# First MLP product as seven block products of block sums, in units of 256 features

## The chip, the cores and the metric

One core of a Trainium2 chip runs the whole program: TensorE (PE) multiplies, VectorE (DVE), ScalarE (ACT) and GpSimd (POOL) work beside it, SyncE (SP) issues the loads. The metric is the device time of one execution in microseconds (us); less is better.

## What is computed

One layer of a hybrid encoder on 512 tokens of 2048 features, in float32:

```python
hn = rms_norm(h, norm_mix_g)
u = hn @ w_pw1 + b_pw1                       # 2048 -> 4096
a, gate = split(u); u = a * sigmoid(gate)
u = depthwise_conv(u, w_dw, width 31) + b_dw
h = h + silu(layer_norm(u)) @ w_pw2 + b_pw2  # 2048 -> 2048
h = h + square(relu(rms_norm(h, norm_ffn_g) @ w_up)) @ w_down   # 2048 -> 8192 -> 2048
out = rms_norm(h, final_norm_g)
```

The change is in the product with `w_up`.

## The kernel before

Features lie on the 128 partitions and tokens along the free axis, so a product is made of matmuls with a 128 x 128 stationary block of weights and 512 moving tokens. For accuracy each float32 operand is split in two parts, `hi` (rounded) and `lo` (the rest), and each block product is three matmuls (`mm3`, L141 to L144): `wh*xh`, `wh*xl`, `wl*xh`. Each of the three has a weight load of its own.

Weights come as a stream of pieces of 512 KB (`pieces`), each 128 partitions x 1024 numbers. `fetch` issues the load of a piece on SP into a buffer `wr`; `split_hi` makes `wh` on ACT (L126), `split_lo` makes `wl` on DVE (L131). The pool has four buffers each of `wr`, `wh` and `wl`. `prep(upto)` does both for all pieces below `upto`.

Phase 1 (to about 390 us) is the first norm, the first pointwise product, the convolution and the LayerNorm. Phase 2 is the second pointwise product and the MLP. There the work is cut into calls of `group`: four output tiles of 128 features in four PSUM banks, over `nk` contraction tiles, two of them per piece, so a piece is 24 matmuls of 512 tokens. Groups use the two halves of the eight banks by turns. While piece p is multiplied, pieces up to p + 2 have been asked for.

After each of the four groups of the second pointwise product, per output tile k: DVE adds the residual (`h`, L781), ACT and DVE split `h` times the gain into `g{k}h` and `g{k}l` (L235, L236), ACT squares `h` (L791), and POOL adds the square to `Q2` (L795). From `Q2` come the token scales `r2` of the norm (`ffn_sum`, `ffn_scale`), which are applied to the product afterwards.

The MLP runs in eight chunks of 1024 hidden features. In each, two groups of 16 contraction tiles give 8 tiles of the hidden layer (relu times `r2` on DVE L818, square on ACT L822, `zh` on ACT L825, `zl` on DVE L826); then four groups of 8 contraction tiles go through `w_down`, and DVE adds each bank to `h` (L837). The last group of the last chunk goes over one half of the tokens and then over the other (`split`), in matmuls of 256 tokens, so that one half's final norm runs under the other's products.

The order on PE is written out by hand. The order on DVE, ACT, POOL and SP in phase 2 is left to a planner: it works with estimated durations, and of the instructions that are ready when an engine comes free it takes the one that is earliest in the program.

Of the kernel before, what the change touches and what calls it, by code (L numbers as in the profile page):

```python
# [24 lines left out]
# columns of the packed per-channel vectors  # L25
# [5 lines left out]
# order and shares of the work among the engines; depthwise taps by ScalarE and GpSimd, and by TensorE; VectorE takes the others  # L31
# [15 lines left out]
FF_CHUNK = 1024  # L47
# [4 lines left out]
def conformer_layer(ctx: ExitStack, tc: tile.TileContext, xT, vecs, wdw, w1, w2, wup, wdn, outT):  # L52
# [4 lines left out]
    wpool = ctx.enter_context(tc.tile_pool(name="wpool", bufs=4))  # L57
# [4 lines left out]
    vec = const.tile([P, 144], F32, name="vec")  # L62
    wd = const.tile([P, NK, CW], F32, name="wd")
# [13 lines left out]

    def col(base, k):
        return vec[:, base + k : base + k + 1]

# [14 lines left out]
    for c in range(DFF // FF_CHUNK):  # L95
        for g in range(FF_CHUNK // 512):
            for k in range(0, NK, 2):
                wide(wup, k * P, c * FF_CHUNK + g * 512)
        for g in range(4):
            for k in range(0, FF_CHUNK // P, 2):  # L100
                wide(wdn, c * FF_CHUNK + k * P, g * 512)

# [15 lines left out]

    def split_hi(i):
        shape = pieces[i][1]  # L120
        r = raws[i]
        pool, bufs = (ph1, 1) if i == n_p1 else (wpool, 4)
        hi = pool.tile(shape, F32R, tag="wh", name=f"wh{i}", bufs=bufs)
        lo = pool.tile(shape, F32R, tag="wl", name=f"wl{i}", bufs=bufs)
        prepped[i] = (hi, lo)
        nc.scalar.copy(out=hi, in_=r)  # L126
# [35 lines left out]
    def spread(dg, out, start=True):  # L162
        """[128 tokens, n] on partitions -> PSUM [128, n * 128], the same on every partition."""
# [20 lines left out]
    def rms_scale(b, name, pool, n=4):  # L184
        """1 / root mean square, tokens on partitions, from the mean squares in b"""
# [6 lines left out]
    # =================== phase 1: norm, pointwise, GLU, depthwise ===================  # L192
# [15 lines left out]
    # the first output pair's operands come, and are split, by contraction tile  # L208
    nc.scalar.dma_start(out=vec, in_=vecs)
    for i in range(4):  # L210
        raws[i] = wpool.tile(pieces[i][1], F32, tag="wr", name=f"wr{i}")
        prepped[i] = tuple(wpool.tile(pieces[i][1], F32R, tag=t, name=f"{t}{i}") for t in ("wh", "wl"))
    state["raw"] = state["prep"] = 4
    for k in range(NK):
# [26 lines left out]
    # The first PRE output pairs take x times the gain, and the norm's scale afterwards; the  # L241
    # others take the normalized x, which is ready by then.
# [3 lines left out]
    # squares of some tiles and their sum by GpSimd, of the others by ScalarE and VectorE  # L246
# [49 lines left out]
    def pw1(j, t0=0, n=T, more=False, hooks=None):  # L296
        pa, pg = bank("mm", f"pa{j}_{t0}")[:, 0:n], bank("mm", f"pg{j}_{t0}")[:, 0:n]
        for k in range(0, NK, 4):
# [3 lines left out]
            for kk in range(4):  # L302
# [3 lines left out]
                if j == 0:  # L306
                    # in the order in which the parts come
# [92 lines left out]
    def early(banks0, banks1):  # L400
        """the normalized x, with the first pairs' GLU and the first convolution between"""
# [33 lines left out]
    def conv_pe(acce, t0, n, i0, i1, npe):  # L435
        """taps i0.. of the npe last ones, of the last tile, on TensorE"""
# [518 lines left out]
```

## Time and profile before

| | |
|---|---|
| time, median of 3 runs | 1995.0 us (1994.71 to 1995.41) |
| span of the profiled execution | 1993.7 us |
| PE busy in the span | 1962.4 us, 98% |
| DVE, ACT, POOL busy | 968.8, 617.1, 387.9 us |
| weights and other data read | 193.27 MB, 99 GB/s with what is written |

The profiled execution has no time of its own beside its span; the median of the timed runs lies 1.3 us above that span. "Busy" counts the time in which an engine had an instruction in work. Matmuls are pipelined: the duration of one (0.39 us for 512 tokens) is longer than the distance from one start to the next, so the pace of PE is read from starts and counts.

### The profile page before, as it was taken

The page shows a single profiled execution, that of the slowest core. Times are in us where ns is not written, and L with a number is a line of the kernel's source. Part 1 is how long each engine was busy: PE and PEld are TensorE (multiplying, and loading weights), DVE is VectorE, ACT ScalarE, POOL GpSimd, SP SyncE. Part 2 cuts the span into 40 slices and gives each one's busy share as a digit, 9 for nine tenths or more (in the row PEclk, how much of TensorE's full clock was granted, in tenths as well). Part 3 has the DMA queues.
Part 4 walks back from the last instruction along what each step waited for, and adds up shares of the span by engine and source line. Part 5 has one row for each costly group of instructions (what it writes and reads, how often), then busy time and mean ns, then how long its engine had stood idle before and what let it go on. Part 6 is the DMA issues. An engine that isn't in the chain of part 4 may idle for free.

```text
span 1993.7 us, 21880 instructions
## 1 busy us (share of the span) xinstructions
PE 1962.4 (98%) x8888; PEld 1629.3 (82%) x8888; DVE 968.8 (49%) x1206; ACT 617.1 (31%) x799; POOL 387.9 (19%) x266
## 2 busy tenths in 40 slices
PE   8899999989999999999999999999999999999997
PEld 5788888978888888888888888888888888888887
DVE  7999999874443332333333233333323333332444
ACT  5533444553322212321221232122213212211332
POOL 6778899851210000000000000000000000000000
PEclk9999999999999999999999999999999999999998
DMA  7233333134233233223323322332332233233222
GB/s 218 76 102 97 92 98 96 54 110 154 96 98 92 99 100 98 95 95 96 98 101 97 95 95 96 97 102 97 96 96 95 96 99 101 95 96 95 96 95 85
DMA packets 155141, 198.88 MB, mean 100 GB/s; under 512 B 7328, under 2 KB 77216, under 8 KB 155040
## 3 DMA queue, kind: packets, MB, share of 16 engines
q1 hardware_dynamic: 154896, 197.42, 31.9%
q8 instruction: 69, 1.13, 0.2%
q14 instruction: 32, 0.26, 0.0%
q10 hardware_dynamic: 144, 0.07, 0.0%
HBM read 193.27 MB, written 4.19 MB: 99 GB/s over the span
## 4 chain that ended last, share of the span: by engine, by line
issue 70%; PE 24%; DVE 3%; DMA 1%; ACT 1%; SPq 0%; POOL 0%; POOLq 0%; DVEq 0%
PE g L143 3%; PE g L142 3%; PE g L144 3%; PE pa L144 2%; PE pa L143 2%; PE pg L144 2%; PE pg L143 2%; PE pg L142 2%; PE pa L142 2%; DMA wr<-w 1%; DVE sl L591 0%; DVE acc L373 0%; DVE wl L131 0%; DMA x<-xT 0%; PE acce L440 0%
## 5 line engine op out<-in xcount | busy, mean ns | idle before, releaser
L131 DVE TENSOR_TENSOR wl<-wr,wh 128x1024 fp32r<-128x1024 f32 x288 | 360.0, 1250 | 888.9 <-ACT wh L126 883.2
L126 ACT CAST wh<-wr 128x1024 fp32r<-128x1024 f32 x348 | 366.1, 1053 | 1175.9 <-PE g L143 1046.7
L142 PE MATMUL g<-zh,wh 128*128 128x512 f32 (+1 forms) x1056 | 404.3, 383 | 0.0
L143 PE MATMUL g<-zl,wh 128*128 128x512 f32 (+1 forms) x1056 | 404.0, 383 | 0.0
L144 PE MATMUL g<-zh,wl 128*128 128x512 f32 (+1 forms) x1056 | 404.0, 383 | 0.0
L189 POOL TENSOR_TENSOR rr_fin<-ms_fin,mhalf 128x2 f32<-128x2 f32 x2 | 1.4, 696 | 1374.2 <-DVE ms_fin L187 1374.2
L373 DVE SCALAR_TENSOR_TENSOR acc<-u,wd,acc 128x512 f32<-128x512 f32 (+1 forms) x362 | 237.4, 730 | 0.2
L142 PEld LDWEIGHTS g<-zh,wh 128*128 128x128 f32 x1056 | 198.4, 188 | 38.8
L143 PEld LDWEIGHTS g<-zl,wh 128*128 128x128 f32 x1056 | 198.4, 188 | 38.7
L144 PEld LDWEIGHTS g<-zh,wl 128*128 128x128 f32 x1056 | 198.4, 188 | 38.7
L131 POOL TENSOR_TENSOR wl<-wr,wh 128x1024 fp32r<-128x1024 f32 x60 | 145.9, 2431 | 40.1 <-ACT wh L126 40.0
L143 PE MATMUL g<-sl,wh 128*128 128x512 f32 (+1 forms) x288 | 107.1, 372 | 6.2 <-DVE sl L591 3.3
L142 PE MATMUL g<-sh,wh 128*128 128x512 f32 (+1 forms) x288 | 107.3, 373 | 0.0
L144 PE MATMUL g<-sh,wl 128*128 128x512 f32 (+1 forms) x288 | 106.3, 369 | 0.0
L837 DVE TENSOR_TENSOR h<-h,g 128x512 f32<-128x512 f32 x124 | 84.6, 687 | 40.8 <-PE g L144 40.8
L362 POOL TENSOR_TENSOR pc<-pc,pm 128x512 f32<-128x512 f32 (+1 forms) x65 | 79.7, 1227 | 3.6 <-ACT pm L360 1.2
L143 PEld LDWEIGHTS g<-sl,wh 128*128 128x128 f32 x288 | 55.2, 192 | 16.3 <-DVE sl L591 4.1
L142 PEld LDWEIGHTS g<-sh,wh 128*128 128x128 f32 x288 | 55.1, 191 | 9.2
L144 PEld LDWEIGHTS g<-sh,wl 128*128 128x128 f32 x288 | 55.3, 192 | 9.0
L360 ACT ACTIVATE pm<-u,wd 128x512 f32<-128x512 f32 (+1 forms) x82 | 53.1, 680 | 20.6 <-POOL pc L362 20.4
L822 ACT ACTIVATE z<-zt 128x512 f32<-128x512 f32 x64 | 40.3, 630 | 53.5 <-DVE zt L818 52.8
L818 DVE SCALAR_TENSOR_TENSOR zt<-g,r 128x512 f32<-128x512 f32 x64 | 43.9, 692 | 22.0 <-PE g L144 21.0
(907 smaller groups left out, 3383.5 us busy)
## 6 DMA issues: line engine op xcount, KB each, us to landing
wr<-wup SPq DMA_DIRECT2D x128, 512.0 KB, 3.8
wr<-wdn SPq DMA_DIRECT2D x128, 512.0 KB, 3.5
wr<-w SPq DMA_DIRECT2D x120, 256.0 KB, 3.3
wr<-w SPq DMA_DIRECT2D x32, 512.0 KB, 3.6
h<-xT SPq DMA_DIRECT2D x4, 1024.0 KB, 11.0
outT<-h SPq DMA_DIRECT2D x14, 256.0 KB, 2.8
x<-xT SPq DMA_DIRECT2D x6, 512.0 KB, 6.2
wr<-w SPq DMA_DIRECT2D x16, 128.0 KB, 5.4
```

Source lines behind the costliest of these rows:

```text
L126: nc.scalar.copy(out=hi, in_=r)
L131: eng.tensor_tensor(out=lo, in0=r, in1=hi.bitcast(F32), op=ALU.subtract)
L142: nc.tensor.matmul(out, lhsT=wh, rhs=xh, start=start, stop=False, **kw)
L143: nc.tensor.matmul(out, lhsT=wh, rhs=xl, start=False, stop=False, **kw)
L144: nc.tensor.matmul(out, lhsT=wl, rhs=xh, start=False, stop=stop, **kw)
L189: nc.gpsimd.tensor_tensor(out=r, in0=ms, in1=mhalf[:, 0:n], op=ALU.pow)
L360: nc.scalar.activation(out=pm, in_=u[:, c : c + n], func=AF.Copy, scale=wd[:, j, c : c + 1])
L362: nc.gpsimd.tensor_add(out=pn, in0=pc[-1], in1=pm)
L373: nc.vector.scalar_tensor_tensor(out=acc if c < end - 1 else vt, in0=u[:, c : c + n], scalar=wd[:, j, c : c + 1], in1=src, op0=ALU.mult, o ...
L818: nc.vector.scalar_tensor_tensor(out=t, in0=banks[m], scalar=0.0, in1=r2, op0=ALU.max, op1=ALU.mult)
L822: nc.scalar.activation(out=z, in_=t, func=AF.Square)
L837: nc.vector.tensor_add(out=h, in0=h, in1=banks[m])
```

## The change

The 2048 x 8192 weight of the first MLP product is worked on in 32 units of 256 hidden features. In each unit the output features, the contraction (pairs of contraction tiles) and the tokens are cut in halves, and the 2 x 2 x 2 block product is made of seven products of block sums and differences in place of eight. A unit has 8 pairs `kt` and for each 7 products, each three matmuls of 256 tokens.

- The sums of the activations are formed once, after the second pointwise product (`form`, `place`): for each of 8 pairs, four DVE operations of 256 columns, one ACT rounding and one DVE subtraction of 7 x 256 columns. They take the place of the split of each tile of `h`. The results for pairs 3 to 7 lie in the space of the second pointwise product's operands, so those for pairs 3 to 5 are written while group 3 runs, those for 6 and 7 behind it. The squares of `h` have one buffer, not two.
- The sums of the weights are formed for each piece (`split_blocks`): three DVE additions more, and the rounding and the subtraction are of 3 + 4 blocks, where they were of one piece. A piece takes two of the three buffers of `wh` and of `wl`; the pool has three buffers, not four (a fourth lives elsewhere in phase 1). The host hands the weights over in the order of the pieces.
- The outputs are put together from the seven products behind each unit (`up`): an ACT copy, four DVE operations that read PSUM, then relu and scale, square, split.
- A unit of the first product prepares one piece ahead (`prep(i0 + p + 2)`). Order: up 0, up 1, up 2, down (0, 1), up 3, up 4, down (2, 3), and so on to down (26, 27), up 29, 30, 31, down (28 to 31). `w_down` goes in 14 jobs of two units and one of four, so DVE adds the banks to `h` 15 times, where it was 8.

```diff
+WBUFS = 3
...
-    wpool = ctx.enter_context(tc.tile_pool(name="wpool", bufs=4))
+    wpool = ctx.enter_context(tc.tile_pool(name="wpool", bufs=WBUFS))
...
+    def split_blocks(i):
+        r = raws.pop(i)
+        s = wpool.tile(BLOCKS, F32, tag="ws", name=f"ws{i}", bufs=1)
+        hr, hs = (wpool.tile([P, 2, n, P], F32R, tag="wh", name=f"wh{i}_{n}", bufs=WBUFS) for n in (3, 4))
+        lr, ls = (wpool.tile([P, 2, n, P], F32R, tag="wl", name=f"wl{i}_{n}", bufs=WBUFS) for n in (3, 4))
+        prepped[i] = (hr, lr), (hs, ls)
+        nc.scalar.copy(out=hr, in_=r[:, :, 1:4])
+        nc.vector.tensor_tensor(
+            out=s[:, :, 0:2], in0=r[:, :, 1:3], in1=r[:, :, 0:1].to_broadcast([P, 2, 2, P]), op=ALU.add
+        )
+        nc.vector.tensor_add(out=s[:, :, 2], in0=s[:, :, 0], in1=r[:, :, 2])
+        nc.vector.tensor_add(out=s[:, :, 3], in0=s[:, :, 2], in1=r[:, :, 3])
+        nc.vector.tensor_tensor(out=lr, in0=r[:, :, 1:4], in1=hr.bitcast(F32), op=ALU.subtract)
+        nc.scalar.copy(out=hs, in_=s)
+        nc.vector.tensor_tensor(out=ls, in0=s, in1=hs.bitcast(F32), op=ALU.subtract)
...
+    OF_RAW = ((3, 3, 0), (6, 0, 0), (4, 1, 0))
+    OF_SUM = ((0, 3, 1), (2, 2, 1), (1, 1, 1), (5, 2, 0))
...
+    def form(kt, b):
+        t1, t2, t3, t4, b11, b12, b21, b22 = (b[:, i] for i in range(8))
+        nc.vector.tensor_sub(out=t3, in0=b12, in1=b22)
+        nc.vector.tensor_sub(out=t1, in0=b22, in1=b21)
+        nc.vector.scalar_tensor_tensor(out=t2, in0=t3, scalar=-1.0, in1=b21, op0=ALU.mult, op1=ALU.subtract)
+        nc.vector.tensor_add(out=t4, in0=t2, in1=b11)
+    def place(kt, b):
+        o = pair_operand(kt)
+        nc.scalar.copy(out=o[:, :, 0], in_=b[:, 0:7])
+        nc.vector.tensor_tensor(out=o[:, :, 1], in0=b[:, 0:7], in1=o[:, :, 0].bitcast(F32), op=ALU.subtract)
...
-                hi, lo = split_scaled(ph2, (f"b{2 * k}", f"b{2 * k + 1}"), f"g{k}", h, col(C_GFFN, k))
...
+            nc.scalar.activation(
+                out=blocks[:, at : at + 2].rearrange("p a b -> p (a b)"), in_=h, func=AF.Copy, scale=col(C_GFFN, k)
+            )
+            sq = ph2.tile([P, T], F32, tag="W", name=f"sqh{k}", bufs=1)
...
+        for p in range(4):
+            prep(i0 + p + 2)
+            for (wh, wl), of in zip(prepped.pop(i0 + p), (OF_RAW, OF_SUM)):
+                for kk in range(2):
+                    kt = 2 * p + kk
+                    for b, (x, q, half) in enumerate(of):
+                        out = banks[q][:, half * HT : half * HT + HT]
+                        xh, xl = T4_OF[kt][:, x, 0], T4_OF[kt][:, x, 1]
+                        first = kt == 0 and (of is OF_RAW or (q, half) == (2, 1))
+                        mm3(out, wh[:, kk, b], wl[:, kk, b], xh, xl, first, kt == 7, skip_group_check=True)
...
+        nc.scalar.copy(out=q1, in_=banks[0][:, 0:HT])
+        nc.vector.tensor_tensor(out=c[:, 2:6:2], in0=two(banks[1]), in1=bc(q1), op=ALU.add)
+        nc.vector.tensor_tensor(out=c[:, 3:6:2], in0=two(banks[2]), in1=bc(c[:, 4]), op=ALU.add)
+        nc.vector.tensor_tensor(out=c[:, 0:2], in0=two(banks[3]), in1=bc(c[:, 5]), op=ALU.subtract)
+        nc.vector.tensor_sub(out=c[:, 3], in0=c[:, 3], in1=banks[3][:, HT:T])
+        t = c[:, 0:4].rearrange("p (m a) t -> p m (a t)", m=2)
+        nc.vector.scalar_tensor_tensor(
+            out=t, in0=t, scalar=0.0, in1=r2[:, None, :].to_broadcast([P, 2, T]), op0=ALU.max, op1=ALU.mult
+        )
+        nc.scalar.activation(out=t, in_=t, func=AF.Square)
...
+        nc.scalar.copy(out=zh, in_=t)
+        nc.vector.tensor_sub(out=zl, in0=t, in1=zh.bitcast(F32))
```

## Rows read from the trace of the kernel before

**Rows 1.** Page, first part: busy us, share of the span, instructions.

```profile
PE 1962.4 (98%) x8888; PEld 1629.3 (82%) x8888; DVE 968.8 (49%) x1206; ACT 617.1 (31%) x799; POOL 387.9 (19%) x266
```

**Rows 2.** Stretches: length, busy us (count) by engine, PE clock, DMA share, GB/s.

```profile
610.00:1955.00 1345.00, 1345.00 (x5936) 1113.70 (x5935) 473.92 (x505) 338.78 (x392) 0.00 (x0) 1.00 0.31 96
1955.00:1984.00 29.00, 27.51 (x224) 27.03 (x222) 14.70 (x31) 12.11 (x26) 3.95 (x4) 0.99 0.22 73
```

**Rows 3.** Waits of PE, 440 to 1994 us, complete: total, times, longest.

```profile
PE sp_fin L164 <- DVE dg_fin L154: 1.5, 1, 1.5
```

**Rows 4.** Order of time on PE, 512 tokens: start, duration; first and last.

```profile
454.62 0.39 PE L143 MATMUL g<-sl,wh 128*128 128x512 f32 x1
...
499.04 0.39 PE L144 MATMUL g<-sh,wl 128*128 128x512 f32 x1
```

**Rows 5.** Order of time on PE, 256 tokens: two stretches, first and last of each.

```profile
411.13 0.28 PE L144 MATMUL g<-sh,wl 128*128 128x256 f32 x1
...
413.05 0.28 PE L142 MATMUL g<-sh,wh 128*128 128x256 f32 x1
...
1955.62 0.28 PE L142 MATMUL g<-zh,wh 128*128 128x256 f32 x1
...
1969.17 0.28 PE L144 MATMUL g<-zh,wl 128*128 128x256 f32 x1
```

**Rows 6.** Page, costliest groups, weight loads: busy us, mean ns, idle before.

```profile
L142 PEld LDWEIGHTS g<-zh,wh 128*128 128x128 f32 x1056 | 198.4, 188 | 38.8
```

**Rows 7.** Groups by line and shape on DVE, 800 to 1800 us.

```profile
L131 DVE TENSOR_TENSOR wl<-wr,wh 128x1024 fp32r<-128x1024 f32 x184 | 225.4, 1225 | 600.2 <-ACT wh L126 598.6
L837 DVE TENSOR_TENSOR h<-h,g 128x512 f32<-128x512 f32 x92 | 62.7, 687 | 30.2 <-PE g L144 30.2
L818 DVE SCALAR_TENSOR_TENSOR zt<-g,r 128x512 f32<-128x512 f32 x48 | 32.9, 692 | 16.5 <-PE g L144 15.8
L826 DVE TENSOR_TENSOR zl<-z,zh 128x512 fp32r<-128x512 f32 x48 | 31.9, 686 | 3.1 <-ACT zh L825 3.1
```

**Rows 8.** The same on ACT, 800 to 1800 us.

```profile
L126 ACT CAST wh<-wr 128x1024 fp32r<-128x1024 f32 x184 | 194.0, 1054 | 715.4 <-PE g L143 715.4
L822 ACT ACTIVATE z<-zt 128x512 f32<-128x512 f32 x48 | 30.2, 630 | 40.1 <-DVE zt L818 39.6
```

**Rows 9.** The same on DVE, whole span: a broadcast operand, and 256 columns.

```profile
L891 DVE TENSOR_TENSOR h<-h,sp_fin 128x512 f32<-128x512 f32 x12 | 7.3, 680 | 0.0
...
L858 DVE TENSOR_TENSOR Q<-Q,sqo 128x256 f32<-128x256 f32 x3 | 1.3, 419 | 0.0
```

**Rows 10.** The same on ACT, whole span: a copy of 256 columns from PSUM.

```profile
L550 ACT COPY mus<-acce 128x256 f32<-128x256 f32 x2 | 0.7, 372 | 5.4 <-PE acce L164 5.4
```

**Rows 11.** Order of time on DVE, behind the last group of the second pointwise product.

```profile
583.10 0.74 DVE L236 SCALAR_TENSOR_TENSOR g12l<-h,vec,g12h 128x512 fp32r<-128x512 f32 x1
...
584.42 1.12 DVE L236 SCALAR_TENSOR_TENSOR g13l<-h,vec,g13h 128x512 fp32r<-128x512 f32 x1
585.47 2.31 DVE L131 TENSOR_TENSOR wl<-wr,wh 128x1024 fp32r<-128x1024 f32 x1
587.70 1.78 DVE L236 SCALAR_TENSOR_TENSOR g14l<-h,vec,g14h 128x512 fp32r<-128x512 f32 x1
```

**Rows 12.** Order of time on POOL in the same stretch.

```profile
583.25 7.38 POOL L795 TENSOR_TENSOR Q<-Q,sqh 128x512 f32<-128x512 f32 x4 [36.13 <-ACT sqh L791]
```

**Rows 13.** Order of time on DVE, behind the first MLP group.

```profile
626.42 2.80 DVE L818 SCALAR_TENSOR_TENSOR zt<-g,r 128x512 f32<-128x512 f32 x4 [1.32 <-PE g L144]
629.14 0.68 DVE L826 TENSOR_TENSOR zl<-z,zh 128x512 fp32r<-128x512 f32 x1
629.95 1.23 DVE L131 TENSOR_TENSOR wl<-wr,wh 128x1024 fp32r<-128x1024 f32 x1
```

**Rows 14.** Waits in the queue of SP, whole span: total, times, longest.

```profile
SPq L115 <- DVE wl L131: 1442.5, 281, 35.9
```

**Rows 15.** Page, loads: count, KB each, median us from issue to landing.

```profile
wr<-wup SPq DMA_DIRECT2D x128, 512.0 KB, 3.8
```

More of the change, by code (lines that the diff above doesn't have):

```diff
@@ L76, in conformer_layer, with hl @@
     nc.vector.memset(mhalf, -0.5)
+    slots = [acts.tile([P, 7, T], F32R, name=f"slot{i}") for i in range(5)]
+    def hl(k):
+        return tuple(slots[n // 7][:, n % 7, :] for n in (2 * k, 2 * k + 1))
     def col(base, k):
@@ L94, in conformer_layer, with up_pieces, down_pieces @@
             wide(w2, k * P, g * 512)
[L95 to L98, printed above, removed]
-        for g in range(4):
-            for k in range(0, FF_CHUNK // P, 2):
-                wide(wdn, c * FF_CHUNK + k * P, g * 512)
+    BLOCKS = [P, 2, 4, P]
+    def up_pieces(u):
+        for p in range(4):
+            pieces.append((wupb[u, p], BLOCKS))
+    def down_pieces(units):
+        for g in range(4):
+            for u in units:
+                wide(wdn, u * UNIT, g * 512)
+    jobs = []
+    for u in range(N_UNITS):
+        jobs.append(("up", u))
+        if u % 2 == 0 and 2 <= u < N_UNITS - 2:
+            jobs.append(("down", (u - 2, u - 1)))
+    jobs.append(("down", tuple(range(N_UNITS - 4, N_UNITS))))
+    for kind, what in jobs:
+        (up_pieces if kind == "up" else down_pieces)(what)
     raws, prepped = {}, {}
@@ L210, in conformer_layer @@
     for i in range(4):
[L211 to L212 removed]
+        raws[i] = wtile(i, "wr", F32)
+        prepped[i] = wtile(i, "wh", F32R), wtile(i, "wl", F32R)
     state["raw"] = state["prep"] = 4
@@ L524, in conformer_layer @@
     mus = ph1.tile([P, T], F32, name="mus", bufs=1)
-    sh = [acts.tile([P, T], F32R, tag=f"a{2 * k}", name=f"sh{k}") for k in range(NK)]
-    sl = [acts.tile([P, T], F32R, tag=f"a{2 * k + 1}", name=f"sl{k}") for k in range(NK)]
+    sh, sl = zip(*(hl(k) for k in range(NK)))
     st = [{}, {}]
@@ L769, in conformer_layer @@
             hooks = dict(zip(LN_AT, (second_sums, second_mean, second_scale)))
+        if g == 3:
+            hooks = {(0, 2 + 2 * i, 0): (lambda kt: lambda: place(kt, blocks_of[kt]))(3 + i) for i in range(3)}
         banks = group(NK, sh, sl, hooks, split=4 if g == 0 else 0)
@@ L795, in conformer_layer @@
                 nc.gpsimd.tensor_add(out=Q2, in0=Q2, in1=sq)
+            if m % 2:
+                form(k // 2, blocks)
+                blocks_of[k // 2] = blocks
+                if k // 2 < 3 or g == 3:
+                    place(k // 2, blocks)
     r2 = const.tile([P, T], F32, name="r2")
@@ L836, in conformer_layer @@
+    Q3 = None
+    for kind, what in jobs[:-1]:
+        if kind == "up":
+            up(what)
+            continue
+        zh, zl = zip(*(t for u in what for t in z_of[u]))
+        for g in range(4):
+            banks = group(2 * len(what), zh, zl)
+            for m in range(4):
                 h = hT[g][:, m, :]
                 nc.vector.tensor_add(out=h, in0=h, in1=banks[m])
-                if end:
-                    sq = ph2.tile([P, T], F32, tag=f"b{k}", name=f"sqo{k}", bufs=1)
-                    nc.scalar.activation(out=sq, in_=h, func=AF.Square)
-                    nc.scalar.activation(out=h, in_=h, func=AF.Copy, scale=col(C_GFIN, k))
-                    if k == 0:
-                        nc.vector.tensor_copy(out=Q3, in_=sq)
-                    else:
-                        nc.vector.tensor_add(out=Q3, in0=Q3, in1=sq)
@@ L848, in conformer_layer, with sq_of @@
-    sqs = [ph2.tile([P, T], F32, tag=f"b{12 + m}", name=f"sqo{12 + m}", bufs=1) for m in range(4)]
+    last_units = jobs[-1][1]
+    zh, zl = zip(*(t for u in last_units for t in z_of[u]))
+    kc = len(zh)
+    Q3 = ph2.tile([P, T], F32, tag="Q2", name="Q3", bufs=1)
+    sqo = [ph2.tile([P, 7, T], F32, tag=f"T{i}", name=f"sqo{i}", bufs=1) for i in range(3)]
+    def sq_of(k):
+        return sqo[k // 7][:, k % 7, :]
+    for g in range(3):
+        banks = group(kc, zh, zl)
+        for m in range(4):
+            k = 4 * g + m
+            h = hT[g][:, m, :]
+            nc.vector.tensor_add(out=h, in0=h, in1=banks[m])
+            sq = sq_of(k)
+            nc.scalar.activation(out=sq, in_=h, func=AF.Square)
+            nc.scalar.activation(out=h, in_=h, func=AF.Copy, scale=col(C_GFIN, k))
+            if k == 0:
+                nc.vector.tensor_copy(out=Q3, in_=sq)
+            else:
+                nc.vector.tensor_add(out=Q3, in0=Q3, in1=sq)
@@ L850, in finish @@
+    sqs = [sq_of(12 + m) for m in range(4)]
     def finish(t0):
```

129 lines of the change are left out of this document (72 added, 57 removed).

## The prediction

> **What bounds the kernel now.** I read the page's first part, then stretches, then who waits. PE is busy for 98% of the span [rows 1], and in the MLP, from 610 to 1955 us, for all of it, at full clock; DVE works there 474 of 1345 us, ACT 339, POOL not at all, and the loads take 0.31 of the DMA engines [rows 2]. From 440 us to the end PE waited for another engine once, 1.5 us in the final norm [rows 3]. So the MLP lasts as long as its matmuls, and fewer of them shorten it as long as the others keep up. "Busy" hides the pace of one matmul. From starts: 44.42 us for 196 steps of 512 tokens, 0.2266 us each [rows 4], which the count of the long stretch repeats (1345 / 5936 = 0.2266) [rows 2]. In two stretches the kernel already runs matmuls of 256 tokens, each with its own weight load: 1.92 us for 16 steps, and 13.55 us for 113, 0.1199 us each [rows 5], while DVE and ACT are at work. Half of 0.2266 would be 0.1133: a half matmul costs 6.6 ns more than half.
>
> **The product.** Removed: 64 output tiles x 16 contraction tiles x 3 = 3072 matmuls, 3072 x 0.2266 = 696.1 us. Added: 32 units x 8 pairs x 7 products x 3 = 5376 of 256 tokens, 5376 x 0.1199 = 644.6 us. Gain 51.5 us, all on the path. Seven eighths would be 87; the price of the halves takes 36 of it. A unit lasts 168 x 0.1199 = 20.1 us, a piece 5.04 (18 matmuls with raw blocks 2.16, 24 with sums 2.88).
>
> A weight load is busy 188 ns by the page [rows 6], more than the step of 120 ns that I use; but each of those steps had one, so loads overlap [rows 5]. The Trainium skill, TensorE: Matmul & The Clock Gate, section Back-to-back issue gap, says that the spacing is set by load and matmul together, and gives 81 ns at 128 tokens and 131 at 512. By that a half matmul would cost (interpolated, an estimate) some three quarters of a whole one, and the product would take about 217 us more in place of 51 less. The trace does not agree: 0.1199 against 0.2266 is 53% [rows 4, 5].
>
> **What DVE and ACT get.** DVE: 1024 numbers 1.225 us, 512 0.69 [rows 7], 256 0.42, and a broadcast operand costs no more (0.68) [rows 9]; 768 I take halfway between 512 and 1024, 0.96. A piece needs 0.69 + 0.42 + 0.42 (sums) + 0.96 + 1.23 (two subtractions) = 3.7 us where it needed 1.23. A unit's outputs need 3 x 0.69 + 0.42 + 1.23 + 1.23 = 4.95. So in a unit of the first product DVE has 4 x 3.7 + 4.95 = 19.8 us of work in 20.1 us of PE. ACT: 1024 1.05, 512 0.63 [rows 8], so 4 x (0.84 + 1.05) + 0.37 [rows 10] + 1.07 + 1.05 = 10 us. In `w_down` a unit lasts 96 x 0.2266 = 21.8 us, with 4 x 1.23 + 8 x 0.69 = 10.4 us on DVE, doubled residual adds included; hidden. On the average DVE keeps up (30.2 of 41.9 us for a unit of both products, 72%); the question is the boundary between two units, where outputs and weights meet.
>
> **A boundary up to up** (17 of the 32 units follow another `up` directly). `wh` has three buffers and a piece takes two; so the raw part of piece 1 can be rounded only when the previous unit's last part is done (call it 0) and is due at 5.04; its sum part from 2.16 on, due at 7.20. Results are there about 0.16 later than PE's step says (0.28 long, 0.12 apart [rows 5]). The planner takes the earliest in the program, which is the outputs: DVE -0.2 to 2.3 the four reads of PSUM, to 3.55 relu and scale; ACT rounds the raw part at 0.2 and squares from 3.6 to 4.65. DVE then has nothing of the outputs that is ready and takes piece 1: rest of its sums (the first fits before 0) to 4.4, raw subtraction to 5.35: PE starts the raw part at 5.4, 0.35 late. ACT rounds z to 5.7, the sums to 6.75; DVE subtracts z to 6.95, sums to 8.2, due at 5.4 + 2.16 = 7.56: 0.65 late. 1.0 us; 1.3 with no sum made beforehand; I take 1.2. Piece 2 then meets its time by about 0.5 us. 17 x 1.2 = 20.4 us. That the planner fills a gap in the outputs with weights shows in the order behind the first MLP group, where a weight subtraction stands between the splits of z [rows 13].
>
> **Other boundaries: nothing.** Up to down: the first down pieces need 1.23 us of DVE per 5.44 us, and two of their buffers come free before the end of the unit. Down to up: pieces 0 and 1 stand ahead of the last adds in the program, due at 5.04; cover 2 us. Banks: the outputs leave them in 2.3 us, next wanted after 10.9 or 20. If that cover failed, 1 us each at 14 places.
>
> **Entry into the MLP.** Before, the last four tiles of `h` were first needed 33 us after their group. Now pairs 6 and 7 are due in piece 3, and piece 2 waits behind their forming on DVE: from 0.8 us (four residual adds done) 0.96 + 1.23 (piece 1), 8 x 0.42 (form), 2 x 2.03 (1792 columns, extrapolated from rows 7), 1.53 + 0.96 (piece 2, raw) = 12.1 us, to 12.9, due at 10.1. POOL adds the squares in the same time, four in 7.38 us [rows 12], and DVE's subtractions beside it went from 0.74 to 1.12 and 1.78, and from 1.23 to 2.31 [rows 11]: 0.4 + 1.1 + 1.0 + 1.0 = 3.5 us lost then, and I add the same. 16.4 - 10.1 = 6.3 us late. Bounds 2.8 (no loss) and 12 (the squares have one buffer, so square and POOL's add alternate, 0.63 [rows 8] + 1.85 [rows 12], and hold up ACT's copies of the later tiles by some 5 us); I take 6.5. In groups 0 to 2 the forming has 43 us of PE as cover, and those for pairs 3 to 5 lie in group 3.
>
> **Queues.** SP issues as many pieces of the same size, 512 KB per 5.04 us in `up` against 5.44. What SP waits for is DVE to release `wr` [rows 14], and a piece lands in 3.8 us [rows 15]: a buffer is refilled three pieces, 15 us, before use, so nothing. The loads of the residual `h` stand behind them by a piece more or less, 43 us of slack. POOL has only the squares. Phase 1 keeps four buffers by another name: nothing, plus or minus 1 us. The end is as it was.
>
> **Sum**, against the span: 1993.7 - 51.5 + 20.4 + 6.5 = 1969.1; the median lies 1.3 above the span: 1970.4, called 1970.
>
> **Rivals.**
> *Cover holds.* DVE makes the sums and the weight subtractions ahead of the outputs, and boundaries cost at most 0.3: 1995.0 - 51.5 + 5 + 3 = 1951, 1946 with nothing at all. For it: DVE has some idle time in the last pieces of a unit. Against: buffers and the one buffer of sums forbid working further ahead.
> *DVE sets the pace (slower).* If the planner leaves all outputs in one run, the subtraction of z included, ahead of piece 1, DVE idles from 3.55 to 5.7 while ACT squares and rounds, and piece 1's raw part comes at 6.95 + 1.53 + 0.96 = 9.4 against 5.04: 4.4 us x 17 = 75, so 1995 - 51.5 + 75 + 6.5 = 2025. It decides from (51.5 - 6.5) / 17 = 2.6 us per boundary. For it: 19.8 of 20.1 us leaves nothing to catch up with, and 5% on DVE's durations is 1 us per unit. Against: the filled gap [rows 13].
> *Stalls eat the gain*: 2.4 to 2.9 us each, 1991 to 1999.
> *The weight load bounds*: if in long runs a half matmul cannot go faster than the 0.188 us of a load [rows 6], 5376 x 0.188 = 1011, 315 us more, 2310. Against it speak both stretches of [rows 5]. The skill's rule above is of this kind, and would give about 2230.
> That the change does not do what it says would be seen in the count of matmuls alone (8888 + 2304 = 11192).
>
> **How the numbers follow.** Forecast (1955 to 1991) 0.53; cover holds 0.20; DVE sets the pace 0.17; eaten 0.08, half of it a little faster or slower than before; weight load 0.02. About 0.2%, 4 us, is what a measurement can tell. Faster by more: 0.53 + 0.20 + 0.02 = 0.75; same 0.05; slower 0.17 + 0.01 + 0.02 = 0.20. The range leaves out the slower cases and the very lowest: 1947 to 1994.
>
> **What would show it.** Right: matmuls of 256 tokens at 0.120 us between the boundaries; PE's waits by `wl` of pieces 1 at about 17 places, 0.3 to 1 us each, in sum some 20 us; one wait of 4 to 8 us about 10 us into the first unit; DVE busy about 1450 us (969 - 128 x 1.23 - 64 x 1.38 - 124 x 0.69 + 32 x 19.8 + 248 x 0.69 + 8), ACT about 740 (617 - 128 x 1.05 - 64 x 1.24 + 32 x 10 + 14). Wrong: waits in every piece (DVE's operations dearer than the rows), waits over 2.6 us at each boundary (the order), or a pace above 0.12 with no wait named.

## The result and the profile after

| | before | after |
|---|---|---|
| time, median, side by side | 1995.2 us | 1961.9 us (1960.9 to 1962.7), 0.9827 of before [0.9814, 0.9841] |
| span of the profiled execution | 1993.7 us | 1959.8 us |
| first MLP matmul to the first of the split group | 582.91 to 1955.62: 1372.7 us | 583.04 to 1922.18: 1339.1 us |

The change gains 33 us (forecast: 25, to 1970). The third line of the table says where: 33.6 of the 33.9 us between the spans lie in the MLP ahead of the split group; phase 1 and the end are as they were.

The page's first part, as in [rows 1]:

```profile
PE 1916.5 (98%) x11192; PEld 1697.3 (87%) x11192; DVE 1408.2 (72%) x1918; ACT 735.6 (38%) x903; POOL 386.5 (20%) x266
```

A long stretch of the MLP, columns as in [rows 2]:

```profile
610.00:1925.00 1315.00, 1309.84 (x8214) 1188.12 (x8213) 894.68 (x1182) 446.76 (x492) 0.00 (x0) 1.00 0.33 100
```

PE is still busy almost all the time and at full clock, with 2304 matmuls more; DVE has gone from 35% [rows 2] to 68% of that stretch. The waits of PE from 440 us to the end of the MLP (columns as in [rows 3]):

```profile
PE u L202 <- DVE wl L186: 5.5, 9, 0.9
PE u L202 <- DVE wl L184: 1.7, 1, 1.7
...
PE u L200 <- ACT wh L185: 1.0, 2, 0.5
```

Against one row before [rows 3], which is still there (the row left out), PE now waits for weights, eleven times for the `lo` or `hi` of block sums (L186, L185) and once for raw blocks (L184): 8.2 us in all, three of the twelve in the first unit. That is less than the 18 us that are missing between the 51.5 us of the product and the 33.6 us measured, so I took the rest from starts. A pair of units, the two `up` of 783 us, first and last of 336 matmuls on PE (start, duration); the next group starts at 824.08:

```profile
783.51 0.28 PE L200 MATMUL u<-T,wh 128*128 128x256 f32 x1
...
823.96 0.28 PE L202 MATMUL u<-slot,wl 128*128 128x256 f32 x1
```

That is 40.57 us, where 336 x 0.1199 = 40.29: a boundary between two units costs 0.3 us here. Twelve of the thirteen pairs lie between 40.57 and 40.59, one at 40.88. The three units in a row at the start and at the end are dearer: the second and third unit, from 610.68, take 45.14 us (4.85 over), the last three, from 1793.32, take 63.56 against 60.43 (3.1 over). Within the last three the second unit is as long as in a pair (20.4), and the third, at 22.97, has the loss. The first unit with the column sums of the squares woven into it lasts from 583.04 to 610.23, 27.2 us; 168 matmuls are 20.1, and the column sums took 0.8 before, so the entry costs 6.2. Together 4.1 + 8.0 + 6.2 = 18.3 us, which is what was given back. The groups of `w_down` are as before, 43.55 us for 192 matmuls, 0.2268 each.

### The profile page after: what moved, and what is told of

The parts are those of the page before. It is cut to its first block, busy times and chain, and to the rows that moved or that the text cites. A ratio compares the mean times of both kernels' runs of the same rounds, so it can differ in the third digit from the quotient of the medians.

```text
span 1959.8 us, 27630 instructions
## 1 busy us (share of the span) xinstructions
PE 1916.5 (98%) x11192; PEld 1697.3 (87%) x11192; DVE 1408.2 (72%) x1918; ACT 735.6 (38%) x903; POOL 386.5 (20%) x266
## 4 chain that ended last, share of the span: by engine, by line
issue 69%; PE 24%; DVE 4%; DMA 1%; ACT 1%; SPq 0%; POOL 0%; POOLq 0%; DVEq 0%
PE g L201 3%; PE g L202 3%; PE g L200 3%; PE pa L202 3%; PE pa L201 3%; PE pg L200 3%; PE pg L202 3%; PE pa L200 3%; PE pg L201 3%; DVE slot L295 1%; DMA wr<-w 1%; DVE acc L432 0%; DVE slot L647 0%; DVE wl L167 0%; DMA x<-xT 0%
## 5 line engine op out<-in xcount | busy, mean ns | idle before, releaser
L200 PE MATMUL g<-z,wh 128*128 128x512 f32 (+1 forms) x1016 | 390.6, 384 | 0.0
L201 PE MATMUL g<-z,wh 128*128 128x512 f32 (+1 forms) x1016 | 390.3, 384 | 0.0
L202 PE MATMUL g<-z,wl 128*128 128x512 f32 (+1 forms) x1016 | 390.1, 384 | 0.0
L202 PE MATMUL u<-slot,wl 128*128 128x256 f32 x1120 | 319.6, 285 | 5.6 <-DVE wl L186 3.7
L200 PE MATMUL u<-slot,wh 128*128 128x256 f32 x1120 | 317.6, 284 | 0.1
L201 PE MATMUL u<-slot,wh 128*128 128x256 f32 x1120 | 317.4, 283 | 0.0
L186 DVE TENSOR_TENSOR wl<-ws,wh 128x1024 fp32r<-128x1024 f32 x128 | 156.8, 1225 | 187.9 <-ACT wh L185 187.0
L185 ACT CAST wh<-ws 128x1024 fp32r<-128x1024 f32 x128 | 134.1, 1048 | 294.7 <-DVE ws L183 138.3
L202 PEld LDWEIGHTS u<-slot,wl 128*128 128x128 f32 x1120 | 215.3, 192 | 9.7 <-DVE wl L186 7.8
L202 PEld LDWEIGHTS g<-z,wl 128*128 128x128 f32 x1016 | 190.9, 188 | 37.8
L200 PEld LDWEIGHTS g<-z,wh 128*128 128x128 f32 x1016 | 190.9, 188 | 37.6
L201 PEld LDWEIGHTS g<-z,wh 128*128 128x128 f32 x1016 | 190.9, 188 | 37.1
L200 PEld LDWEIGHTS u<-slot,wh 128*128 128x128 f32 x1120 | 215.4, 192 | 0.4 <-ACT wh L185 0.3
L201 PEld LDWEIGHTS u<-slot,wh 128*128 128x128 f32 x1120 | 215.4, 192 | 0.0
L202 PE MATMUL u<-T,wl 128*128 128x256 f32 x672 | 190.7, 284 | 1.9 <-DVE wl L186 1.8
L200 PE MATMUL u<-T,wh 128*128 128x256 f32 x672 | 190.7, 284 | 1.0 <-ACT wh L185 1.0
L201 PE MATMUL u<-T,wh 128*128 128x256 f32 x672 | 190.1, 283 | 0.0
```

The lines of the kernel that those rows point to most:

```text
L185: nc.scalar.copy(out=hs, in_=s)
L186: nc.vector.tensor_tensor(out=ls, in0=s, in1=hs.bitcast(F32), op=ALU.subtract)
L200: nc.tensor.matmul(out, lhsT=wh, rhs=xh, start=start, stop=False, **kw)
L201: nc.tensor.matmul(out, lhsT=wh, rhs=xl, start=False, stop=False, **kw)
L202: nc.tensor.matmul(out, lhsT=wl, rhs=xh, start=False, stop=stop, **kw)
```

## The experiments

All ratios are to the kernel before, in runs on the same chip, with 95% intervals. The theory was that of the prediction: a matmul of 256 tokens costs 6.6 ns more than half of one of 512, DVE's order at the boundary decides what the boundaries cost, and the entry is late by what DVE has to form.

**1. The price of the halves alone (`halves`).** The kernel before, with each matmul of the first MLP product done as two of 256 tokens, and nothing else changed:

```diff
+                if halve:
+                    for tok in (slice(0, HT), slice(HT, T)):
+                        mm3(
+                            banks[m][:, tok],
+                            wh[:, kk, c],
...
+                    continue
```

> The kernel before, but each matmul of the first MLP product is done in two of 256 tokens, 6144 in place of 3072; nothing else changes. Theory (a half matmul takes 0.1199 us also in runs of 40 us and more): 3072 x (2 x 0.1199 - 0.2266) = 40.6 us more, 2036. Rival (in a long run a weight load's 0.188 us bounds it): 3072 x (0.376 - 0.2266) = 459 us more, 2454. Rival (half the columns cost half): 1995.

2036.5 us against 1996.1, 1.0201 [1.0186, 1.0217]: 40.4 us for 3072 matmuls, 13.1 ns for each that was split in two, so 6.6 ns per half. Its long stretch:

```profile
610.00:1990.00 1380.00, 1380.00 (x8880) 1265.03 (x8880) 471.99 (x502) 336.35 (x390) 0.00 (x0) 1.00 0.31 94
```

PE has no gap, at full clock, with a weight load per half and DVE and ACT as lightly loaded as in [rows 2]. So the 0.1199 us that I had from two short stretches holds in long runs, and the rival that a load bounds a half matmul at 0.188 us falls. The Trainium skill's spacing (TensorE: Matmul & The Clock Gate, section Back-to-back issue gap), read as the prediction read it, has a half matmul at three quarters of a whole one, 0.17 us, and would make this run some 350 us longer than the kernel before, an estimate (3072 x (2 x 0.17 - 0.2266)). The trace does not agree.

**2. What the block sums of the weights cost (`no_sums`).** The three additions on DVE are left out, and the raw blocks stand in for the sums, so the output is not the reference's:

```diff
-        nc.vector.tensor_tensor(
-            out=s[:, :, 0:2], in0=r[:, :, 1:3], in1=r[:, :, 0:1].to_broadcast([P, 2, 2, P]), op=ALU.add
-        )
-        nc.vector.tensor_add(out=s[:, :, 2], in0=s[:, :, 0], in1=r[:, :, 2])
-        nc.vector.tensor_add(out=s[:, :, 3], in0=s[:, :, 2], in1=r[:, :, 3])
...
+        nc.scalar.copy(out=hs, in_=r)
+        nc.vector.tensor_tensor(out=ls, in0=r, in1=hs.bitcast(F32), op=ALU.subtract)
```

> The changed kernel without the three DVE additions that form the sums of the weights (the raw blocks are rounded and split in their place; the output is not the reference's). DVE has 4 x 1.53 = 6.1 us less to do per unit of the first product, PE the same. Theory (the 18 us that the MLP takes beyond its matmuls are waits for DVE): most of them go, 1945 to 1951. Rival (they lie in PE's pace between 512 and 256 tokens or in the loads): 1961.

1948.3 us, 0.9761 [0.9746, 0.9775]; by the ratios 13 us less than the changed kernel. Pairs take 40.31 us and the last three units 60.47 (40.29 and 60.43 would be no loss), and of PE's waits for weights one is left, in the first unit:

```profile
PE u L196 <- DVE wl L178: 1.8, 1, 1.8
```

So nearly all that the boundaries cost goes with DVE's additions, 1.5 us per piece (0.69 + 2 x 0.42). The edit takes away their time and also ACT's wait for them, and the run does not tell the two apart. This is where "cover holds" (1951) would have been.

**3. DVE's order at the boundary (`outputs_first`, `program_order`).** Both write out the order on DVE and ACT by hand for each run of `up` calls. `outputs_first` is the order that the prediction worked out: the outputs up to relu and scale, then piece 1's raw blocks, then the rest of the outputs. `program_order` is that of its rival: all outputs, then piece 1.

```diff
+            if run is None:
+                run = tc.manual_schedule(engines={mybir.EngineType.DVE, mybir.EngineType.Activation})
+                run.__enter__()
             up(what)
...
+        if run:
+            run.__exit__(None, None, None)
```

For `outputs_first`, square and split of the outputs are also put off (`rest`) until the raw subtraction of the next piece has been issued:

```diff
         nc.vector.tensor_tensor(out=lr, in0=r[:, :, 1:4], in1=hr.bitcast(F32), op=ALU.subtract)
+        flush()
...
+        def rest():
+            nc.scalar.activation(out=t, in_=t, func=AF.Square)
...
+        late.append(rest)
```

> The changed kernel with DVE and ACT held, in runs of units of the first product, to the order that the prediction assumed: all reads of PSUM, relu and scale, then the sums and the raw subtraction of piece 1, then the rest of the outputs, then the subtraction of the sums. Theory (the prediction had the price of that order right, and the planner found a better one): about 1.2 us at 17 boundaries in place of 10 us in all, so 1970 to 1978. Rival (the order does not matter, buffers and durations do): 1962, within 2.

1972.9 us, 0.9883 [0.9868, 0.9897]. A pair takes 41.40 us, 1.1 over, where I had put 1.2. PE's waits in the MLP, all of one kind (the longest is in the first unit):

```profile
PE u L210 <- DVE wl L184: 18.4, 18, 5.1
```

DVE at one boundary (start, duration; L943 to L948 are the outputs, L179 to L184 the sums and the raw subtraction of piece 1, L960 the subtraction of z):

```profile
720.73 0.69 DVE L943 TENSOR_TENSOR c<-u,q 128x512 f32<-128x512 f32 x1 [0.36 <-PE u L210]
...
723.31 1.23 DVE L948 SCALAR_TENSOR_TENSOR c<-c,r 128x1024 f32<-128x1024 f32 x1
...
725.98 0.95 DVE L184 TENSOR_TENSOR wl<-wr,wh 128x768 fp32r<-128x768 f32 x1
726.85 1.22 DVE L960 TENSOR_TENSOR z<-c,z 128x1024 fp32r<-128x1024 f32 x1
```

> The changed kernel with DVE and ACT held to program order in runs of units of the first product: all of a unit's outputs, the split of z included, ahead of piece 1 of the next unit. Theory (order at the boundary is what decides; the prediction's slower rival): 4.4 us at 17 boundaries, 75 in place of 10, so 2020 to 2030, slower than the kernel before. Rival (DVE catches up within the unit, or later pieces hide it): under 1985.

2060.9 us, 1.0329 [1.0311, 1.0346]: slower than before, as the rival had it, and 36 us past its 2025. The boundary at 824 us, on DVE:

```profile
823.07 1.23 DVE L940 SCALAR_TENSOR_TENSOR c<-c,r 128x1024 f32<-128x1024 f32 x1
826.50 1.22 DVE L951 TENSOR_TENSOR z<-c,z 128x1024 fp32r<-128x1024 f32 x1 [2.20 <-ACT z L950]
...
829.16 0.95 DVE L184 TENSOR_TENSOR wl<-wr,wh 128x768 fp32r<-128x768 f32 x1
```

The same boundary in stretches of 4 us, columns as in [rows 2]:

```profile
826.00:830.00 4.00, 0.50 (x2) 0.30 (x2) 3.43 (x5) 1.87 (x3) 0.00 (x0) 0.97 0.00 0
830.00:834.00 4.00, 3.83 (x21) 3.83 (x22) 3.60 (x6) 1.50 (x3) 0.00 (x0) 0.61 0.48 131
```

DVE stands idle for 2.20 us behind the scale, as forecast, and PE waits 1.63 us for `wh` and 2.58 for `wl`: 4.2 us, where the prediction had 4.4. What the forecast lacked comes behind the wait: from 830 to 834 us the granted clock is 0.61 and PE starts 21 matmuls where 33 fit (4 / 0.12). A pair lasts 46.0 to 47.3 us, so a boundary 5.7 to 7.0.

What the planner made of it in the changed kernel, DVE at the boundary inside the pair of 783 us (L935 to L938 read PSUM, L940 is relu and scale, L951 the subtraction of z):

```profile
803.69 0.68 DVE L935 TENSOR_TENSOR c<-u,q 128x512 f32<-128x512 f32 x1
804.29 0.68 DVE L179 TENSOR_TENSOR ws<-wr 128x512 f32<-128x512 f32 x1
804.89 0.95 DVE L184 TENSOR_TENSOR wl<-wr,wh 128x768 fp32r<-128x768 f32 x1
805.76 0.68 DVE L936 TENSOR_TENSOR c<-u,c 128x512 f32<-128x512 f32 x1
806.36 0.41 DVE L182 TENSOR_TENSOR ws<-ws,wr 128x256 f32<-128x256 f32 x1
806.70 0.68 DVE L937 TENSOR_TENSOR c<-u,c 128x512 f32<-128x512 f32 x1
...
807.96 1.22 DVE L940 SCALAR_TENSOR_TENSOR c<-c,r 128x1024 f32<-128x1024 f32 x1
```

Piece 1's raw subtraction (L184) stands behind the first read of PSUM, 1.2 us after it; in `outputs_first` it stands 5.25 us after (720.73 to 725.98). Each further read of PSUM needs the one ahead of it, and the planner has filled the places between with additions for the weights (L179, L182). That it did so because of that dependence is inferred; no run tried another planner.

**4. The entry into the MLP (`after_again`, `entry_no_squares`).** The changed kernel once more, beside a version that leaves out the squares of the last four tiles of `h` (on ACT) and their adds (on POOL), so that its output is not the reference's:

```diff
+            if g < 3:
                 sq = ph2.tile([P, T], F32, tag="W", name=f"sqh{k}", bufs=1)
                 nc.scalar.activation(out=sq, in_=h, func=AF.Square)
```

> The changed kernel once more, as the measure for the other runs of this set: 1962, within 2.

> The changed kernel without the squares of the last four tiles of the residual and GpSimd's four adds of them (the norm's scale leaves those features out, so the output is not the reference's). Theory (in the entry into the MLP, VectorE's operations are held up beside GpSimd's adds, by 0.3 + 1.1 + 1.1 + 1.1 = 3.6 us in the trace of the changed kernel, and PE's waits of 1.9, 1.0 and 0.9 us in the first unit come of that): 2 to 4 us less, 1958 to 1960. Rival (VectorE's own work between the last group and piece 2 is late without them, 2.8 us by the prediction's lower bound): less than 1 us.

1964.2 us, 0.9839 [0.9826, 0.9853], and 1959.2, 0.9815 [0.9802, 0.9829]: 5 us less, a little more than expected. The first unit went from 27.2 us to 23.7; 1.3 us of the rest lie ahead of the first MLP matmul (584.32 and 583.00 us), where the edit does not reach. The rows below are those of the first measurement of the changed kernel, which has the same waits; DVE in the first unit:

```profile
586.69 1.52 DVE L839 TENSOR_TENSOR blocks<-blocks 128x256 f32<-128x256 f32 x1
...
590.88 2.01 DVE L846 TENSOR_TENSOR slot<-blocks,slot 128x1792 fp32r<-128x1792 f32 x1
592.82 1.50 DVE L182 TENSOR_TENSOR ws<-ws,wr 128x256 f32<-128x256 f32 x1
594.23 0.95 DVE L184 TENSOR_TENSOR wl<-wr,wh 128x768 fp32r<-128x768 f32 x1
595.10 3.10 DVE L846 TENSOR_TENSOR slot<-blocks,slot 128x1792 fp32r<-128x1792 f32 x1
```

POOL beside it, with the idle time before and what ended it:

```profile
586.41 1.52 POOL L884 TENSOR_TENSOR Q<-Q,sqh 128x512 f32<-128x512 f32 x1 [1.80 <-ACT sqh L880]
591.67 2.35 POOL L884 TENSOR_TENSOR Q<-Q,sqh 128x512 f32<-128x512 f32 x1 [3.75 <-ACT sqh L880]
```

PE, two matmuls that follow each other:

```profile
593.23 0.28 PE L201 MATMUL u<-slot,wh 128*128 128x256 f32 x1
595.23 0.39 PE L202 MATMUL u<-slot,wl 128*128 128x256 f32 x1 [1.72 <-DVE wl L184]
```

Stretches of 2 us, columns as in [rows 2]:

```profile
593.00:595.00 2.00, 0.51 (x5) 0.31 (x3) 2.00 (x2) 0.81 (x2) 1.26 (x2) 1.00 0.00 0
595.00:597.00 2.00, 1.77 (x10) 1.77 (x11) 2.00 (x2) 0.00 (x0) 1.32 (x1) 0.68 0.00 0
597.00:599.00 2.00, 2.00 (x12) 2.00 (x11) 1.54 (x2) 0.37 (x1) 0.00 (x0) 0.50 0.00 0
```

PE waits for piece 2's raw `wl`, 1.88 us beyond its pace (593.23 to 595.23). DVE made it behind the splitting of pair 6 (590.88) and behind an addition of 256 columns that took 1.50 us beside POOL's add, where 0.42 is its time alone [rows 9]. Without the squares these rows of DVE last 0.41 and 2.01 us, that wait is gone, and the first 102 matmuls take 12.24 us in place of 15.39. The clock did not fall there either. So 3.5 us of the entry (27.2 - 23.7) come of the squares and POOL's adds and of what followed from them. What is left is 2.8 us (23.7 - 20.1 - 0.8); PE's waits in it are above all for what DVE forms, the longest 1.0 us, so I put it down to DVE's own work.

**5. A better order (`pairs`, and four more).** Three units in a row were dearest (4.85 and 3.1 us); the theory was that DVE's work has not been caught up when a third unit follows. `pairs` never runs more than two `up` without a `down` between them:

```diff
-        if u % 2 == 0 and 2 <= u < N_UNITS - 2:
-            jobs.append(("down", (u - 2, u - 1)))
+        if u % 2 and u < N_UNITS - 2:
+            jobs.append(("down", (0,) if u == 1 else (u - 2,) if u == N_UNITS - 3 else (u - 2, u - 1)))
```

> The changed kernel with another order of jobs: never three units of the first product in a row (down of unit 0 alone behind up 1, then down 1 and 2 behind up 3, and so on, down 27 alone behind up 29). Theory (a second boundary behind a first costs 2.2 us where one alone costs 0.3, since VectorE hasn't caught up): about 4 to 5 us less, 1957 to 1958. Rival (one unit of the second product alone gives VectorE no time for its 16 more adds, and the loss moves there): 1962 or more.

1958.1 us, 0.9807 [0.9794, 0.9821], 6.1 less than `after_again`, on the same chip. Yet its first unit is longer, 29.4 us (582.58 to 611.98) against 27.2, with a new wait, the longest of PE's:

```profile
PE cs_ffn L234 <- POOL Q L884: 3.2, 1, 3.2
```

POOL at that time:

```profile
585.95 1.52 POOL L884 TENSOR_TENSOR Q<-Q,sqh 128x512 f32<-128x512 f32 x1 [1.79 <-ACT sqh L880]
591.23 5.80 POOL L884 TENSOR_TENSOR Q<-Q,sqh 128x512 f32<-128x512 f32 x1 [3.76 <-ACT sqh L880]
```

DVE beside it:

```profile
590.42 2.01 DVE L846 TENSOR_TENSOR slot<-blocks,slot 128x1792 fp32r<-128x1792 f32 x1
592.36 0.41 DVE L182 TENSOR_TENSOR ws<-ws,wr 128x256 f32<-128x256 f32 x1
592.69 0.94 DVE L184 TENSOR_TENSOR wl<-wr,wh 128x768 fp32r<-128x768 f32 x1
593.56 2.01 DVE L846 TENSOR_TENSOR slot<-blocks,slot 128x1792 fp32r<-128x1792 f32 x1
```

The operations of DVE stand in the same order as in the changed kernel, and the two that took 1.50 and 3.10 us there now take 0.41 and 2.01. POOL's one add lasts 5.80 us instead, until they are through, and the column sums on PE wait for it.

`pairs_places` moves the splitting of pairs 6 and 7 behind the preparing of piece 2's weights in the program; `pairs_sum` asks for the column sums 24 matmuls later:

```diff
-                if u == 0 and p == 2 and of is OF_RAW:
+                if u == 0 and p == 2 and of is OF_SUM:
                     ffn_sum()
```

> As pairs, and the rounding and subtraction of the last two pairs of operands stand behind the weights of piece 2 in the program, not ahead of them. Theory (piece 2 is what PE waits for in the entry, the pairs are due a piece later): 1 to 2 us less than pairs, 1955 to 1957. Rival (VectorE's work up to piece 3 is the same, so the wait only moves a piece on): as pairs, within 0.7.

> The changed kernel as the measure for the other runs of this set: 1962 to 1964.

> As pairs, but the column sums of the squares stand on PE behind the sum part of piece 2 of the first unit, 2.88 us of matmuls later. In the trace of pairs PE waited 3.2 us for GpSimd's last add, and its clock then went to half for about 6 us. Theory (the wait and the lower clock behind it are the price of the place of these sums): 3 to 5 us less than pairs, 1953 to 1956. Rival (the wait turns up at the spread of the scale behind the unit, or at the weights of the next pieces): as pairs, 1957 to 1959.

`pairs_places`: 1958.2 us, 0.9811 [0.9797, 0.9824], no gain; PE's waits are those of `pairs`, down to the 3.2 us for POOL. But the edit did not do what it was meant to do: the planner put DVE's operations in the same order as in `pairs` (L846 at 592.53, L182 at 594.47, L184 at 594.80, L846 at 595.67), with the splitting of pair 6 still ahead of piece 2's raw subtraction. So this run tests neither its theory nor its rival. `pairs_sum`: 1957.5, 0.9809 [0.9795, 0.9822]; beside it `after_third` had 1964.4, 0.9840 [0.9826, 0.9853]. PE no longer waits for POOL itself, but a wait of 2.8 us for `wh` of piece 2's sums (L185) has come in its place. On ACT this rounding stands behind the last square, which waits for POOL's add to release the one buffer of squares:

```profile
598.77 0.63 ACT L880 ACTIVATE sqh<-h 128x512 f32<-128x512 f32 x1 [4.34 <-POOL Q L884]
599.30 1.03 ACT L185 CAST wh<-ws 128x1024 fp32r<-128x1024 f32 x1
```

That add lasts 5.81 us here, and without it the rounding could have begun at 597.6, when DVE had made the sums, 1.7 us earlier. So a better place for the column sums does not do away with the cost of that add, part of which reaches PE by way of ACT.

`pairs_dve` is `pairs_sum` with the last four adds of squares on DVE, so that POOL is out of the entry:

```diff
-                nc.gpsimd.tensor_add(out=Q2, in0=Q2, in1=sq)
+                (nc.vector if g == 3 else nc.gpsimd).tensor_add(out=Q2, in0=Q2, in1=sq)
```

> As pairs_sum, and VectorE in place of GpSimd adds the squares of the last four tiles, 4 x 0.69 = 2.8 us more work on VectorE. Theory (VectorE and GpSimd hold each other up in the entry by 3.6 us on one side or 4 to 5 us on the other): entry the same or up to 1 us shorter, 1952 to 1956, and no operation of VectorE of 256 columns over 0.45 us there. Rival (VectorE's work is what is late in the entry): 2 to 3 us more than pairs_sum.

1955.4 us, 0.9798 [0.9784, 0.9811], 9.0 less than `after_third` and 2.1 less than `pairs_sum`, whose runs (1956.97 to 1958.53) all lie above its own (1954.62 to 1956.43). DVE's forming runs at 0.42 us per operation throughout, the four adds cost 0.68 each. The longest of PE's waits:

```profile
PE u L200 <- ACT wh L185: 3.1, 1, 3.1
```

A stretch of 2 us behind it, columns as in [rows 2]:

```profile
602.00:604.00 2.00, 2.00 (x11) 2.00 (x11) 0.98 (x3) 0.87 (x1) 0.00 (x0) 0.50 0.00 0
```

The clock is at half behind that single wait of 3.1 us. `pairs_dve_places` tries to spread it: piece 2's preparation and then the splitting of pairs 6 and 7 in a fixed order on DVE.

```diff
+            if u == 0 and p == 1:
+                with tc.manual_schedule(engines={mybir.EngineType.DVE}):
+                    prep(i0 + p + 2)
+                    place(6, blocks_of[6])
+                    place(7, blocks_of[7])
```

> As pairs_dve, and VectorE is held to do all of piece 2 of the first unit's weights ahead of the two subtractions of 1792 columns for the last pairs of operands. In the trace of pairs_dve PE waited 3.1 us for the sums of that piece, whose last addition stood behind both. Theory (the order in the entry, not the amount of work, is what is left there): 2 to 4 us less than pairs_dve, 1951 to 1954. Rival (the pairs are then late for piece 3 by as much): 1955, within 1.

1954.4 us (1952.6 to 1959.8), 0.9793 [0.9778, 0.9807]. The gain of 2 to 4 us was not there: the interval overlaps with that of `pairs_dve`, and the first two units last 48.6 us against 48.3 there. Its waits:

```profile
PE u L202 <- DVE wl L186: 2.3, 4, 0.8
PE u L200 <- ACT wh L185: 1.8, 2, 1.3
```

Several small ones in place of one. DVE is busy for 16.10 of the 17 us from 583 to 600. From this I infer that the amount of its work sets the entry now and that its order only moves the waits; no run took work off DVE here. By the ratios (0.9793 and 0.9798 against 0.9827 to 0.9840) both of the last two are 6 to 9 us faster than the changed kernel; between the two no difference was shown.

## Why the prediction was right, and where not

The forecast of 1970 lies 8.5 us above the measured 1961.9, and one term has nearly all of it: the boundaries, with 8.3.

**The product, right.** 51.5 us removed; the pace was 0.1199 us in the first unit (583.04 to 593.23, 85 steps) and in `halves`. It was taken from two short stretches [rows 5], against the page's 188 ns of a weight load [rows 6]: steps with a load each are the better evidence, since loads overlap.

**The boundaries, a term too large.** 20.4 us were put, about 12 measured. The step that failed is "The planner takes the earliest in the program, which is the outputs". In fact the planner put piece 1's raw subtraction between the reads of PSUM. With the order that the prediction assumed a boundary does cost 1.1 us (`outputs_first`; 1.2 put), with the planner's own 0.3. So the sign that was named for being right, waits at about 17 places for `wl` of piece 1, some 20 us in sum, did not come: behind the boundaries PE waited nine times, each time for block sums and never for raw blocks. The row that would have told was among those quoted: it fills a gap with weights [rows 13], and I used that only for the gap behind the relu.

That one price was then multiplied by 17. Thirteen boundaries between two `down` jobs cost 0.3. Of the four in the runs of three units one cost 0.3 too, and the other three 2.0 to 2.8; `pairs` removed the runs of three and gained 6 us. The prediction's rival said that 19.8 us of DVE work per unit of 20.1 "leaves nothing to catch up with". The direction is borne out, since the loss comes where no `down` follows, but DVE is not full there. The third unit of the last three, columns as in [rows 2]:

```profile
1833.90:1856.87 22.97, 21.18 (x170) 20.37 (x169) 18.60 (x25) 10.04 (x12) 0.00 (x0) 1.00 0.33 95
```

DVE has 4.4 us without work in it. Whether buffers or the order of the operations make PE wait there, no run shows.

**The entry, right in sum, not in kind.** 6.5 us put, 6.2 measured. The losses to POOL are there (0.42 us going to 1.50, 2.01 to 3.10), but the planner took piece 2 between the two pairs, so one wait of 4 to 8 us became 1.88, 1.04 and 0.91 us. Another 1.7 us is the clock, which the prediction did not have: 13 matmuls at 0.214 us, and the column sums, which took 1.30 us where they had taken 0.81. `entry_no_squares` gives the prediction's two numbers, 2.8 us without any loss to POOL and 3.5 with it, but of the 3.5 about half is the clock and not waiting, so the agreement is in part luck.

**The rival "DVE sets the pace", right in kind, short in price.** In `program_order`, which gives DVE the rival's order, its waits came to 4.2 of the 4.4 us forecast; the clock behind them adds 1.5 us or more, so 2061 and not 2025. The point from which the gain is lost, 2.6 us per boundary, would then be reached at a shorter wait than the prediction said; no run shows at which.

**The rest.** DVE busy 1408 us (about 1450 put), ACT 736 (740), 11192 matmuls as counted. DVE's durations were those put, by line and shape from 800 to 1800 us (columns as in [rows 7]):

```profile
L184 DVE TENSOR_TENSOR wl<-wr,wh 128x768 fp32r<-128x768 f32 x95 | 90.7, 955 | 12.2 <-ACT wh L178 10.6
L179 DVE TENSOR_TENSOR ws<-wr 128x512 f32<-128x512 f32 x94 | 64.7, 689 | 6.3 <-DMA wr<-wupb 4.7
L182 DVE TENSOR_TENSOR ws<-ws,wr 128x256 f32<-128x256 f32 x95 | 40.1, 422 | 2.0
...
```

The 768 columns, put halfway between 512 and 1024 at 0.96 us, took 0.955. Queues, other boundaries, banks and the end cost nothing that shows, as put: no row among PE's waits names a load.

## What to carry to other kernels

Price a scheme that saves multiplications by the start-to-start pace of the smaller matmuls, from a stretch that has them with their loads: here half the tokens cost 53%, and 51.5 us were left of the 87 that an eighth would be. Then look at the engine that makes the block sums, unit by unit and not by its mean share of 72%: here the units of one kind follow each other without loss to speak of by twos and with 2 to 2.8 us by threes, so a unit of the other kind belongs behind every second one. Ask of the planner where it puts the operation that the next wait hangs on, and look whether an edit moved it at all. And read the granted clock behind each of PE's long waits before counting it at its length.

## What was not expected of the hardware

**The clock behind a wait.** In the MLP of these runs, each time that PE had stood idle for 1.7 us or more, its granted clock was found at half (1.2 of 2.4 GHz) for 3.4 us or more, from some time in the wait or up to 2.2 us behind it. In the changed kernel the idle time of 1.72 us ends at 595.23, the clock is at half from 595.7 to 599.2, and matmuls are 0.213 us apart. In `pairs_dve` a wait of 3.1 us ends at 599.45, and the clock is at half from 598.2 to 605.1. In `program_order` idle times of 1.47 and 2.41 us, two matmuls between them, end at 830.17, with half the clock from 829.7 to 833.1, and a fall like it comes at each boundary. In `outputs_first` a wait of 5.1 us ends at 598.77, and the granted clock is 0.51 in the four us after it. The waits of up to 1.3 us in `pairs_dve_places` left it at 1.00.

The trace before had such cases already, ahead of the 440 us from which [rows 3] lists PE's waits: an idle time, and the clock in a stretch behind it (columns as in [rows 2]).

```profile
404.02 0.39 PE L143 MATMUL g<-sl,wh 128*128 128x256 f32 x1 [2.27 <-DVE sl L591]
406.36:409.77 3.41, 3.41 (x16) 3.23 (x16) 1.33 (x5) 0.47 (x2) 0.71 (x1) 0.50 0.07 27
```

Nor does the length of one wait decide. The idle time of 2.96 us that ends at 429.04 before the change has half the clock behind it from 430.25 to 433.66; the same one in the changed kernel has the full clock behind it:

```profile
429.99 0.50 PE L201 MATMUL g<-slot,wh 128*128 128x512 f32 x1 [2.96 <-DVE slot L660]
429.99:433.40 3.41, 3.03 (x12) 2.17 (x12) 3.41 (x7) 0.82 (x1) 2.66 (x2) 1.00 0.47 145
```

**DVE and POOL hold each other up, and which one loses can turn.** Beside POOL's adds, operations of DVE with two operands in SBUF took 1.1 us longer (0.41 to 1.50, 2.01 to 3.10). With the same operations in the same order, in `pairs` and `pairs_sum`, those two lost nothing and one add of POOL took 5.80 and 5.81 us, where an add alone takes 1.3. The Trainium skill, SBUF — State Buffer, section Who interferes with whom, says that a DVE instruction with two SBUF inputs contends with a GpSimd instruction that reads SBUF, and that the order of issue decides who is blocked. The trace agrees that they contend. What turned it here stays open: POOL's add starts 0.79 us behind DVE's subtraction in the changed kernel (591.67 and 590.88) and 0.81 us in `pairs` (591.23 and 590.42), with DVE's next operation behind both times, and still DVE is held up in the one and POOL in the other.
